# A column mean whose last row groups are added by another split of the engines: group 61 by GpSimd and TensorE, and VectorE held behind a store

## The chip, the cores, the metric

One core of one Trainium2 chip. The metric is the device time of one execution in microseconds; every kernel here computes the mean of each column of an 8192 x 8192 fp32 array.

## The reference

```python
def setup_inputs():
    return {"x": np.random.randn(8192, 8192).astype(np.float32)}

def reference(x):
    return np.mean(x, axis=0)
```

## The kernel before

The rows form 64 groups of 128; a group is a tile of 128 partitions and 8192 columns. Five engines work side by side: SyncE issues the loads into four row buffers, VectorE adds groups into `acc`, at the end TensorE sums over the partitions by multiplying with a tile of 1/8192, GpSimd takes over some late additions, and ScalarE copies sums out. The columns are 16 blocks of 512 (`F`); TensorE's sums of blocks 0 to 14 go to four banks of PSUM (the memory into which it adds), the last, the "edge", to a tile of its own. "Landed" means that all semaphore signals of a transfer have come; a "record" is one instruction's entry in the trace. For the last three groups the work is shared out, so that little is left to do when the last bytes land:

```python
    add(acc[:, 6 * F:], acc[:, 6 * F:], r61[:, 6 * F:], [load(r61[:, 4 * F:], rows(g)[:, 4 * F:])])  # VectorE
    g += 1
    load(r62, rows(g))
    tc.keep_in_program_order(nc.gpsimd.tensor_add(                                                  # GpSimd
        out=acc[:, 13 * F:], in0=acc[:, 13 * F:], in1=r62[:, 13 * F:]))
    g += 1
    for lo, hi in [(0, 9), (9, 12), (15, 16)]:
        load(r63[:, lo * F:hi * F], rows(g)[:, lo * F:hi * F])

    plan = [                      # TensorE, in this order: source, from block, to block
        (ahead, 12, 15),          # group 63, loaded early
        (acc, 0, 6),
        (head, 0, 4),             # group 61, loaded early
        (r61, 4, 6),
        (acc, 6, 13),             # waits for VectorE's part of 61
        (r62, 0, 13),
        (acc, 13, 16),            # waits for GpSimd's part of 62
        (r63, 0, 9),
        (r63, 9, 12),
        (r63, 15, 16),
    ]
    # ... one matmul per block; block i goes to column group i % 4 of the array and to bank i // 4

    copy(res[:96, 3, :], banks[3][:96, :])                       # ScalarE
    s3 = store(nc.scalar, out[12 * F:15 * F]..., res[0:96:32, 3, :], loads[-3])
    for b in range(3):
        copy(res[:, b, :], banks[b][:])                          # ScalarE
    nc.vector.tensor_copy(out=resedge[:], in_=edge[:])           # VectorE
    # ... SyncE waits for the loads
    store(nc.sync, out[:8 * F]..., res[0:P:32, 0:2, :])          # SyncE's first store: banks 0 and 1
    # ... SyncE waits for s3 and the last loads
    store(nc.sync, out[8 * F:12 * F]..., res[0:P:32, 2, :])      # SyncE's last store: bank 2
    store(nc.scalar, out[15 * F:]..., resedge[0:P:32, :])        # the edge store
```

Of the kernel before, what the change touches and what calls it, by code (L numbers as in the profile page):

```python
# [9 lines left out]
def kernel(  # L10
# [2 lines left out]
    x: bass.AP,  # L13
    out: bass.AP,
):




# [17 lines left out]
    nc = tc.nc  # L37
    f32 = mybir.dt.float32
    M, N = x.shape
    P = nc.NUM_PARTITIONS  # L40
    F = 512
# [4 lines left out]
    sync = mybir.DependencyInfo(mybir.DependencyClass.Sync, mybir.DependencyReason.DATA)  # L46
# [6 lines left out]
    acc = bufs[:, U - 1, :]  # L53
# [18 lines left out]
    def load(dst, src):  # L72
        ins = tc.keep_in_program_order(nc.sync.dma_start(out=dst, in_=src)).ins
        k = len(loads)
        over = loads[k - 8:k - 6] if k >= 8 and k % 2 == 0 else []
        tc.declare_no_dep(ins, group="loads", keep=over, reason="the reader of the buffer waited")
        for o in over:
            tc.add_manual_dep(ins, o.name, sync, reason="covers the next load too")
        tc.add_to_no_dep_group("loads", ins)
        loads.append(ins)  # L80
        return ins

    def rows(g, n=1):
        return x[g * P:(g + n) * P, :]

    def load_rows(g, u, n):
        return load(bufs[:, u:u + n, :], rows(g, n).rearrange("(p j) c -> p j c", j=n))
# [3 lines left out]
    def add(dst, a, b, dmas):  # L91

        ins = nc.vector.tensor_add(out=dst, in0=a, in1=b).ins  # L93
        if dmas and adds:
            waiter = nc.scalar if len(adds) % 8 > 1 else nc.gpsimd
            nop = joins[waiter] = tc.keep_in_program_order(waiter.nop()).ins  # L96
            for o in dmas + adds[-1:]:
                tc.add_manual_dep(nop, o.name, sync, reason="the no-op waits")
            for group in ("loads", "adds"):
                tc.declare_no_dep(ins, group=group, reason="the no-op waited")  # L100
            tc.add_manual_dep(ins, nop.name, sync, reason="waits for both at once")
        elif adds:
            tc.declare_no_dep(ins, group="loads", reason="the add ahead waited")
        tc.add_to_no_dep_group("adds", ins)
        adds.append(ins)
# [9 lines left out]
    g = 6  # L115
    while g < G - 10:
        u = (g + 2) % 4
        dma = load_rows(g, u, 2)
        add(both, bufs[:, u, :], bufs[:, u + 1, :], [dma])
        add(acc, acc, both, [])  # L120
        g += 2
    while g < G - 3:
        row = bufs[:, (g + 2) % 4, :]
        add(acc, acc, row, [load(row, rows(g))])
        g += 1
    r61, r62, r63 = [bufs[:, (g + 2 + j) % 4, :] for j in range(3)]
    add(acc[:, 6 * F:], acc[:, 6 * F:], r61[:, 6 * F:], [load(r61[:, 4 * F:], rows(g)[:, 4 * F:])])
    g += 1
    load(r62, rows(g))
    tc.keep_in_program_order(nc.gpsimd.tensor_add(  # L130
        out=acc[:, 13 * F:], in0=acc[:, 13 * F:], in1=r62[:, 13 * F:]))
    g += 1
    for lo, hi in [(0, 9), (9, 12), (15, 16)]:
        load(r63[:, lo * F:hi * F], rows(g)[:, lo * F:hi * F])

    plan = [
        (ahead, 12, 15),
        (acc, 0, 6),
        (head, 0, 4),
        (r61, 4, 6),  # L140
        (acc, 6, 13),
        (r62, 0, 13),
        (acc, 13, 16),
        (r63, 0, 9),
# [5 lines left out]
    for row, lo, hi in plan:  # L150
        base = 12 * F if row is ahead else 0
        for i in range(lo, hi):
            for q in range(4) if i == NBLK else [i % 4]:
                c = i * F + (q * W if i == NBLK else 0)
                dst = edge if i == NBLK else banks[i // 4]
                tc.keep_in_program_order(nc.tensor.matmul(  # L156
                    out=dst[32 * q:32 * q + 32, :],
# [10 lines left out]
    resedge = sb.tile([P, W], f32, name="resedge")  # L168
# [4 lines left out]
    def store(engine, dst, src, *then):  # L173
        ins = tc.keep_in_program_order(engine.dma_start(out=dst, in_=src)).ins
        for o in then:
            tc.add_manual_dep(ins, o.name, sync, reason="follows that load")
        return ins
# [12 lines left out]
    landed(loads[-2], s3)  # L190
    landed(loads[-1], adds[-1])
    store(nc.sync, out[8 * F:12 * F].rearrange("(q c) -> q c", q=4), res[0:P:32, 2, :])
    store(nc.scalar, out[15 * F:].rearrange("(q c) -> q c", q=4), resedge[0:P:32, :])


# [28 lines left out]
```

## Time and profile before

| | before |
|---|---|
| time | 630.02 us (median of 6 runs, 629.82 to 630.25) |
| span of the profile | 628.05 us |
| read from memory | 268.44 MB at 427 GB/s |
| VectorE's part of group 61 | 609.54 to 615.03 us |
| GpSimd's part of group 62 | 615.55 to 619.02 us |
| group 63, blocks 0 to 8, landed | 620.89 us |
| last store issued, landed | 624.57, 627.21 us |

All times inside an execution are us from the start of the span. The prediction below shows and reads the page, the chain and the timeline of this kernel. One part of the page it does not show, and that turned out to matter: the list of the DMA queues (packets, MB, share of the 16 engines' span).

### The profile page before, as it was taken

The numbers are of one execution on the slowest core, as the hardware profiler recorded it, in microseconds if no ns is written. First come the engines' busy times: TensorE is split into PE (matmuls) and PEld (weight loads), VectorE is DVE, ScalarE is ACT, GpSimd is POOL, SyncE is SP. The second block draws the span as 40 slices with busy tenths as digits, with TensorE's granted clock in tenths as the row PEclk, the third lists the DMA queues (packets, MB, share of the 16 engines' span).
The fourth block names the chain that finished last, engine by engine and source line by source line (L and its number), as shares of the span: only waits on it lengthen the run. The fifth ranks groups of instructions, "written<-read, shape, count | busy, mean of one in ns | idle before, by whom it ended". The sixth has DMA issues, their size and how long they took to land.

```text
span 628.1 us, 453 instructions
## 1 busy us (share of the span) xinstructions
PE 16.3 (3%) x114; PEld 5.7 (1%) x114; DVE 527.0 (84%) x60; ACT 3.7 (1%) x6; POOL 4.0 (1%) x7
## 2 busy tenths in 40 slices
PE   0000100000000000000000000000000000000017
PEld 0000000000000000000000000000000000000002
DVE  0019999999888998888988889888899888999991
ACT  0000000000000000000000000000000000000001
POOL 0000000000000000000000000000000000000002
PEclk9999999999999999999999999999999999999999
DMA  9999999999999999999999999999999999999996
GB/s 401 417 451 402 449 455 413 455 413 455 413 455 413 455 413 447 422 442 426 438 430 438 430 430 438 426 442 413 455 405 463 401 467 401 434 434 434 432 434 256
DMA packets 5924, 268.50 MB, mean 428 GB/s; under 512 B 655, under 2 KB 659, under 8 KB 1058
## 3 DMA queue, kind: packets, MB, share of 16 engines
q1 hardware_dynamic: 5908, 268.46, 99.0%
q8 instruction: 1, 0.02, 0.0%
q10 hardware_dynamic: 14, 0.01, 0.0%
q14 instruction: 1, 0.01, 0.0%
HBM read 268.44 MB, written 0.03 MB: 427 GB/s over the span
## 4 chain that ended last, share of the span: by engine, by line
DMA 55%; DVE 33%; another core or an unknown queue 10%; PE 0%; issue 0%; ACT 0%; ACTq 0%; POOLq 0%; POOL 0%
DMA bufs<-in_x_dram 55%; DVE bufs L93 33%; PE bank L156 0%; ACT bufs L171 0%; ACTq L96 0%; POOLq L96 0%; POOL ready L60 0%; POOL ones L57 0%; POOLq L208 0%
## 5 line engine op out<-in xcount | busy, mean ns | idle before, releaser
L93 DVE TENSOR_TENSOR bufs<-bufs 128x8192 f32<-128x8192 f32 (+2 forms) x59 | 526.7, 8927 | 88.3 <-DMA bufs<-in_x_dram 44.3
L156 PE MATMUL bank<-bufs,ones 128*32 128x512 f32 x84 | 12.7, 662 | 542.3 <-DVE bufs L93 542.0
L156 PEld LDWEIGHTS bank<-bufs,ones 128*32 128x32 f32 x84 | 4.2, 117 | 550.4 <-DVE bufs L93 544.4
L184 DVE COPY resedge<-edge 128x128 f32<-128x128 f32 x1 | 0.3, 291 | 9.1 <-PE edge L156 9.1
L130 POOL TENSOR_TENSOR bufs<-bufs 128x1536 f32<-128x1536 f32 x1 | 3.5, 3471 | 614.4 <-DMA bufs<-in_x_dram 614.4
L171 ACT COPY bufs<-bank 128x512 f32<-128x512 f32 (+1 forms) x4 | 2.2, 586 | 620.0 <-PE bank L156 620.0
L156 PE MATMUL bank<-ahead,ones 128*32 128x512 f32 x6 | 1.9, 1056 | 65.5 <-DMA ahead<-in_x_dram 65.5
L156 PE MATMUL bank<-head,ones 128*32 128x512 f32 x8 | 3.3, 990 | 0.0
L156 PE MATMUL edge<-bufs,ones 128*32 128x128 f32 x16 | 1.7, 274 | 0.0
L114 ACT ACT_TABLE_LOAD x1 | 1.3, 1283 | 0.7 <-PEq L208 0.7
L156 PEld LDWEIGHTS edge<-bufs,ones 128*32 128x32 f32 x16 | 1.0, 109 | 0.9 <-DMA bufs<-in_x_dram 0.5
L156 PEld LDWEIGHTS bank<-ahead,ones 128*32 128x32 f32 x6 | 0.2, 138 | 65.5 <-issue 65.5
L156 PEld LDWEIGHTS bank<-head,ones 128*32 128x32 f32 x8 | 0.6, 159 | 1.3 <-issue 1.3
L114 ACT COPY warm<-ones 128x32 f32<-128x32 f32 x1 | 0.2, 218 | 0.0
L60 POOL TENSOR_TENSOR ready<-ones 128x1 f32<-128x1 f32 x1 | 0.2, 193 | 0.1
L57 POOL MEMSET ones<- 128x32 f32 x1 | 0.1, 125 | 0.3 <-POOLq L208 0.3
L208 POOL MEMSET const-bfloat16-1.0<- 128x1 bf16 x1 | 0.1, 102 | 0.0
L208 POOL MEMSET const-uint8-127<- 128x1 uint8 x1 | 0.1, 102 | 0.0
L208 POOL MEMSET const-float32-0.0<- 128x1 f32 x1 | 0.1, 98 | 0.2 <-issue 0.2
L208 POOL MEMSET const-float32-1.0<- 128x1 f32 x1 | 0.1, 98 | 0.0
## 6 DMA issues: line engine op xcount, KB each, us to landing
bufs<-in_x_dram SPq DMA_DIRECT2D x8, 4096.0 KB, 22.3
bufs<-in_x_dram SPq DMA_DIRECT2D x1, 3072.0 KB
bufs<-in_x_dram SPq DMA_DIRECT2D x1, 2304.0 KB, 20.2
head<-in_x_dram SPq DMA_DIRECT2D x1, 1024.0 KB, 4.8
ahead<-in_x_dram SPq DMA_DIRECT2D x1, 768.0 KB
bufs<-in_x_dram SPq DMA_DIRECT2D x1, 768.0 KB, 21.7
bufs<-in_x_dram SPq DMA_DIRECT2D x26, 29.9
bufs<-in_x_dram SPq DMA_DIRECT2D x1, 256.0 KB, 21.9
```

Source lines behind the costliest of these rows:

```text
L57: nc.gpsimd.memset(ones[:], 1.0 / M)
L60: nc.gpsimd.tensor_add(out=ready[:], in0=ones[:, 0:1], in1=ones[:, 1:2]))
L93: ins = nc.vector.tensor_add(out=dst, in0=a, in1=b).ins
L114: tc.keep_in_program_order(nc.scalar.copy(out=warm[:], in_=ones[:]))
L130: tc.keep_in_program_order(nc.gpsimd.tensor_add(out=acc[:, 13 * F:], in0=acc[:, 13 * F:], in1=r62[:, 13 * F:]))
L156: tc.keep_in_program_order(nc.tensor.matmul(out=dst[32 * q:32 * q + 32, :], lhsT=ones[:], rhs=row[:, c - base:c - base + (W if i == NBLK e ...
L171: tc.keep_in_program_order(nc.scalar.copy(out=dst, in_=src))
L184: nc.vector.tensor_copy(out=resedge[:], in_=edge[:])
L208: nc = _bacc.Bacc("TRN2", target_bir_lowering=False, num_devices=1)
```

## The change

The intent: VectorE is free after group 60; GpSimd adds blocks 9 to 15 of group 61 and then, as before, its part of group 62; TensorE adds blocks 4 to 8 of group 61 directly. And VectorE's stream of instructions ends behind the store of the edge.

```diff
+    def late_add(row, lo):
+        tc.keep_in_program_order(nc.gpsimd.tensor_add(
+            out=acc[:, lo * F:], in0=acc[:, lo * F:], in1=row[:, lo * F:]))
...
-    add(acc[:, 6 * F:], acc[:, 6 * F:], r61[:, 6 * F:], [load(r61[:, 4 * F:], rows(g)[:, 4 * F:])])
+    load(r61[:, 4 * F:], rows(g)[:, 4 * F:])
+    late_add(r61, 9)
     g += 1
     load(r62, rows(g))
-    tc.keep_in_program_order(nc.gpsimd.tensor_add(
-        out=acc[:, 13 * F:], in0=acc[:, 13 * F:], in1=r62[:, 13 * F:]))
+    late_add(r62, 13)
...
-        (acc, 0, 6),
+        (acc, 0, 9),
         (head, 0, 4),
-        (r61, 4, 6),
-        (acc, 6, 13),
+        (r61, 4, 9),
+        (acc, 9, 13),
...
-    store(nc.scalar, out[15 * F:]..., resedge[0:P:32, :])
+    last = store(nc.scalar, out[15 * F:]..., resedge[0:P:32, :])
+    hold = tc.keep_in_program_order(nc.vector.nop()).ins
+    tc.add_manual_dep(hold, last.name, sync, reason="VectorE ends with the last store")
```

## The prediction

> **What bounds the kernel now.** I read the page first (busy table, slices, DMA queues), then the chain of waits, then the timeline of each engine in the last 30 us, since the change touches nothing earlier.
>
> ```profile
> span 628.1 us, 453 instructions
> PE 16.3 (3%) x114; PEld 5.7 (1%) x114; DVE 527.0 (84%) x60; ACT 3.7 (1%) x6; POOL 4.0 (1%) x7
> DMA  9999999999999999999999999999999999999996
> HBM read 268.44 MB, written 0.03 MB: 427 GB/s over the span
> ```
>
> The input is 8192 x 8192 x 4 bytes = 268.4 MB, read once. The DMA row is full until the last slice. VectorE is busy 84% and looks like the bound, but it is not: the chain of waits goes through transfers for 55% of the span and through VectorE for 33% only because a pair's two adds follow its landing. So only the tail can move: what lies between the last landings (620.9 to 623.4) and 628.1. The end of the chain:
>
> ```profile
> 600.66 20.22 DMA bufs<-in_x_dram
> 620.89 0.14 issue
> 621.02 2.90 PE bank L156 x24
> 623.92 0.02 issue
> 623.94 0.58 ACT bufs L171
> ```
>
> Columns are start, length, what. Blocks 0 to 8 of group 63 land at 620.89, TensorE adds them at once, ScalarE copies the last bank to 624.52; the two last stores, the ends and the final barrier make the other 3.5 us. This is the path that the change must shorten or may lengthen. Beside it, in the timeline:
>
> ```profile
> 591.94 23.09 DVE L93 TENSOR_TENSOR bufs<-bufs 128x8192 f32<-128x8192 f32 x3
> 615.55 3.47 POOL L130 TENSOR_TENSOR bufs<-bufs 128x1536 f32<-128x1536 f32 x1 [614.42 <-DMA bufs<-in_x_dram]
> 620.62 0.58 ACT L171 COPY bufs<-bank 96x512 f32<-96x512 f32 x1 [618.37 <-PE bank L156]
> 621.23 1.27 ACTq L174 DMA_DIRECT2D out_dram<-bufs  x1
> 622.54 1.07 ACT L171 COPY bufs<-bank 128x512 f32<-128x512 f32 x2 [1.34 <-PE bank L156]
> 623.94 0.58 ACT L171 COPY bufs<-bank 128x512 f32<-128x512 f32 x1 [0.32 <-PE bank L156]
> ```
>
> VectorE adds groups 59, 60 and then the part of 61, ending at 615.03. GpSimd adds three blocks and the edge of group 62 until 619.02; with it TensorE finishes bank 3, ScalarE copies that at 620.62, issues its store for 1.27 us, and reaches banks 0, 1 at 622.54, with no time in between. Before the last copy it has only 0.32 us of slack. So GpSimd's end stands some 0.4 us off the binding path, no more.
>
> [...] 3471/1536 = 2.26 ns a column against 5492/5120 = 1.07 (groups by form), a factor 2.1. [...] here the two never overlap, for VectorE's last add ends before GpSimd may start. [...] consecutive passes of one column group start 0.85 us apart at 609.5 to 613.8 and 0.43 us apart later, so the rate doubled some 4.5 us after the start. [...]
>
> **The change, part by part.**
>
> Removed: VectorE's one add of 5120 columns, 5.49 us (609.54 to 615.03). VectorE then ends with group 60 at 609.45. No load waits for the removed add (the last loads are issued at 601.5, and the built programs show the same waits on the queue), so no transfer starts earlier. Gain on the path: 0.
>
> Added on GpSimd: an add of 3584 columns (blocks 9 to 15) ahead of the old one. It may start when group 60 is added; group 61 landed at 605.7 (its semaphore). The old GpSimd add began 0.16 us after the last thing it waited for, so start 609.45 + 0.15 = 609.6. Duration: 3584 x 2.26 = 8.1 us with no fixed cost; less a fixed part, taken from the 193 ns of the one-column add, (3471 - 193) / 1535 = 2.14 ns a column and 0.2 + 7.65 = 7.85 us[...]. I take 7.85: end 617.45. The old add follows after a semaphore wait of about 0.1 us and takes 3.47 us: end **621.0 instead of 619.02**, 2.0 us later. VectorE did it in half the time; that is the heart of the matter.
>
> Added on TensorE: 3 blocks of acc and 3 of r61 more (18 instead of 12 before the long wait). Blocks go to four column groups that run side by side; the fullest has 6 blocks. Estimate: 2.65 blocks at 1.7 us until the rate doubles at 614, 3.35 at 0.86: idle by 616.9, before GpSimd's 617.5. Off the path. From 617.5 it must do acc 9 to 12 and the 13 blocks of r62: for the groups that hold blocks 13 and 14 that is 4 blocks, 3.45 us, ready at 620.95; so both arrive together with GpSimd at 621.07. In the kernel before these groups were free only at about 619.4 to 619.5, 0.4 us after GpSimd; that slack is used up. Two passes on, and 0.17 us of completion: bank 3 is done at 621.07 + 0.43 + 0.59 + 0.17, some 622.3. Column group 0 has five blocks, free at 621.8, edge to about 622.1: group 63, which had begun at 621.02, begins at 622.2. By the spacing of before (1.10, 1.96 and 2.8 us from that start to banks 0, 1, 2) the banks are done at 623.3, 624.2, 625.0; before, 622.1, 623.0, 623.9. TensorE alone makes +1.1 us.
>
> ScalarE: copy of bank 3 at 622.3 instead of 620.62 (+1.7), store issued at 622.9. If the issue again takes 1.27 us, the copies of banks 0 and 1 start at 624.2 and 624.7, end at 625.3, and SyncE's first store follows at 625.3 instead of 623.64; it takes 0.70, the waits behind it 0.22, and the last store starts at 626.2 instead of 624.57: **+1.66 us**. If the issue takes only 0.6 us, as the same queue's second store did, TensorE sets the pace: copies end at 624.8, the last store starts at 625.7: +1.15 us. Behind it landing (2.64 us from issue) and barrier stay as they are.
>
> The hold on VectorE: no instruction of its own; the built program puts the wait on VectorE's last branch. The edge store landed at 627.03, SyncE's last at 627.21, and SyncE goes on to 627.34 before the barrier fires. VectorE must be released and drained by then; it has 0.3 us and drains took 0.01 to 0.03 us. After the change the edge store goes out earlier still against the last one. Worth 0, give or take 0.2.
>
> Sum: 0 + (1.15 to 1.66) + 0 us, I take **+1.5 us: 630.2 + 1.5 = 631.7 us**, slower by a quarter of a per cent.
>
> **The rivals.** First, GpSimd stays hidden: the tail is set by the landing of group 63 alone, and the time is 630.2. For it speaks that the chain names only the transfer ahead of TensorE; against it that the slack is 0.4 us and the shift 2.0. Second, TensorE falls back to half rate in its idle stretch from 616.9 to 617.5 (for some column groups from 616). Then the work from 617.5 doubles: the groups reach block 13 at 624.4 rather than 620.95, and the time is near 635. [...] Third, the hold costs or gives something behind the barrier, where the profile shows nothing: the measured 630.2 is 2.1 us over the span. I see no mechanism for more than some tenths.
>
> **Range and chances.** The low end is the hidden case plus a little, 630.6; the high end +1.66 with GpSimd 0.3 us slower, a late doubling and the difference between chips, 633.0. Two per cent are 12.6 us, and the whole tail behind the last landing is under 5: faster 0.01, slower 0.01, within 2% 0.98.
>
> **What would show it.** GpSimd's wide add at 609.6 for about 7.85 us, its narrow one ending near 621.0; the bank 3 copy at 622.3 with GpSimd, not TensorE's backlog, as the last wait; the ACT store's issue length; group 63's matmuls starting at 622.2 although it still lands at 620.9; the last store at 625.7 to 626.2; a span of 629.2 to 629.7. Wrong if that last store starts within 0.3 us of 624.57, if the passes behind 617.5 are 0.85 us apart, or if the span and the time move by different amounts.

The sum came to 0 + (1.15 to 1.66) + 0 us, taken as +1.5, and the 7.85 us of the wide add rest on the trace's 2.14 ns a column. One term of the range is 0.3 us for a late doubling, an estimate from no run, which the high end of 633.0 counts in. In the paragraph that begins with 3471/1536, the 2.26 ns a column are GpSimd's and the 1.07 VectorE's. Of the second rival's premise, that TensorE's rate can fall to half again, the trace of before shows one case: its clock record stands at 1.00 from 614.12 to 627.77 and at 0.50 behind, 3.7 us after TensorE's last pass ended (624.10). Whether an idle stretch of 0.6 us, as forecast here, is enough it does not show.

## More of the kernel before

```profile
q1 hardware_dynamic: 5908, 268.46, 99.0%
q8 instruction: 1, 0.02, 0.0%
q10 hardware_dynamic: 14, 0.01, 0.0%
q14 instruction: 1, 0.01, 0.0%
```

Two packets are of the kind that the page names `instruction`, no data; they are read here as an engine's fetches of its instructions. They count for nothing in the shares. When they run is not on the page. By the trace's packet records q8's runs from 622.18 to 623.28, before the last two stores move; q14's is the one that matters below.

## The result, and the profile after

The changed kernel takes **630.41 us** (median of 6 runs, 630.21 to 630.79), the kernel before 630.02 in the same rounds: 0.39 us more, where 1.5 were predicted; the predicted range began at 630.6. Ratios in this document are the mean time of one kernel's fast runs over that of the other's in the same rounds, so not quite the ratio of the medians; here it is 1.0007, 95% interval 0.9994 to 1.0020. By the time alone the two kernels are not told apart. Their traces, however, differ in two large steps of opposite sign.

The first step is the predicted one. Groups by form of the kernel after (columns: line, engine, operation, tiles, form, count, then busy us and mean ns, then idle us before it):

```profile
L123 POOL TENSOR_TENSOR bufs<-bufs 128x3584 f32<-128x3584 f32 x1 | 7.8, 7770 | 608.5 <-DVE bufs L92 608.5
L123 POOL TENSOR_TENSOR bufs<-bufs 128x1536 f32<-128x1536 f32 x1 | 3.5, 3471 | 0.1
```

They run from 609.60 to 620.91, as predicted to a tenth. ScalarE's part of the timeline of the kernel after (start, length):

```profile
622.07 0.58 ACT L175 COPY bufs<-bank 96x512 f32<-96x512 f32 x1 [619.82 <-PE bank L160]
622.68 1.27 ACTq L178 DMA_DIRECT2D out_dram<-bufs  x1
624.00 1.56 ACT L175 COPY bufs<-bank 128x512 f32<-128x512 f32 x3 [1.34 <-PE bank L160]
```

Bank 3 is copied at 622.07 instead of 620.62, the store behind it is issued for the same 1.27 us, and the three other copies now follow each other without a gap. The chain of the kernel after names TensorE, where the chain before named the transfer:

```profile
600.83 8.70 DVE bufs L92
609.53 0.04 issue
609.57 11.73 PE bank L160 x69
...
622.24 1.76 PE bank L160 x12
624.00 0.91 ACT bufs L175 x2
624.90 0.05 issue
624.96 0.60 ACT bufs L175
```

It does so because TensorE is hardly idle from 609.57 on; which of its waits matters the chain doesn't say (pool_late and pe_part bear on it). SyncE's last store, in the timelines of before and of after:

```profile
624.57 0.56 SPq L174 DMA_DIRECT2D out_dram<-bufs  x1
```

```profile
626.01 0.56 SPq L178 DMA_DIRECT2D out_dram<-bufs  x1
```

It is issued 1.45 us later. So far the prediction holds (1.15 to 1.66). But the span grew by 0.53 us only (628.05 to 628.59), and the barrier behind the store costs the same. The second step is the landing, counted from a store's issue to its last semaphore signal: the store issued at 624.57 landed at 627.21, that at 626.01 landed at 627.74, 2.64 against 1.72 us (from unrounded times, as in the table below). The edge store before took 2.55 us to land, after 1.82. The DMA queues in the 0.8 us in which the parts of these last two stores move, before (625.6 to 626.4) and after (626.7 to 627.5), show what shares the engines with them:

```profile
q14 instruction: 1, 0.01, 3.9%
q1 hardware_dynamic: 8, 0.01, 3.5%
q10 hardware_dynamic: 8, 0.00, 1.2%
```

```profile
q1 hardware_dynamic: 10, 0.01, 3.6%
q10 hardware_dynamic: 8, 0.00, 1.3%
```

q1 carries SyncE's store, q10 the edge store, q14 an instruction fetch of 8192 bytes. Before, it runs from 625.68 to 626.18, in the midst of the stores: by the packet records three of the edge store's four parts start at 625.71 to 625.73, the fourth at 626.18, when the fetch is done. Its semaphore arrives 0.82 us after its last packet, the last store's 0.91 us; after the change these are 0.38 and 0.33. So where the fetch runs, one part of the edge store starts late and both semaphores come late. What delays the semaphores is not shown; which of the 16 engines carried which packet the packed trace does not tell. After the change, the fetch starts at 628.63, when the stores have landed and the span (628.59) has just ended.

### The profile page after: what moved, and what is told of

It reads as the page before. It is cut to its first block, busy times and chain, and to the rows that moved or that the text cites. A ratio compares the mean times of both kernels' runs of the same rounds, so it can differ in the third digit from the quotient of the medians.

```text
span 628.6 us, 466 instructions
## 1 busy us (share of the span) xinstructions
PE 17.4 (3%) x120; PEld 5.7 (1%) x120; DVE 521.5 (83%) x59; ACT 3.6 (1%) x6; POOL 11.8 (2%) x8
## 4 chain that ended last, share of the span: by engine, by line
DMA 52%; DVE 35%; another core or an unknown queue 10%; PE 2%; ACT 0%; issue 0%; ACTq 0%; POOLq 0%; POOL 0%
DMA bufs<-in_x_dram 52%; DVE bufs L92 35%; PE bank L160 2%; ACT bufs L175 0%; ACTq L95 0%; POOLq L95 0%; PE edge L160 0%; POOL ready L59 0%; POOL ones L56 0%; POOLq L214 0%
## 5 line engine op out<-in xcount | busy, mean ns | idle before, releaser
L92 DVE TENSOR_TENSOR bufs<-bufs 128x8192 f32<-128x8192 f32 (+1 forms) x58 | 521.2, 8986 | 88.3 <-DMA bufs<-in_x_dram 44.3
L160 PE MATMUL bank<-bufs,ones 128*32 128x512 f32 x90 | 15.2, 694 | 542.0 <-DVE bufs L92 542.0
L123 POOL TENSOR_TENSOR bufs<-bufs 128x3584 f32<-128x3584 f32 (+1 forms) x2 | 11.2, 5620 | 608.5 <-DVE bufs L92 608.5
```

Source lines behind the costliest of these rows:

```text
L92: ins = nc.vector.tensor_add(out=dst, in0=a, in1=b).ins
L123: tc.keep_in_program_order(nc.gpsimd.tensor_add(out=acc[:, lo * F:], in0=acc[:, lo * F:], in1=row[:, lo * F:]))
L160: tc.keep_in_program_order(nc.tensor.matmul(out=dst[32 * q:32 * q + 32, :], lhsT=ones[:], rhs=row[:, c - base:c - base + (W if i == NBLK e ...
```

## The experiments

Theory A, formed from the two traces: VectorE's end triggers the fetch some 1.4 us later (by the records, 1.2 us behind the edge copy before and 1.3 us behind the waiting branch after), and the hold moves it behind the stores. The rivals were B, that the stores landed late before only because they were issued 0.09 us apart (after: 0.60); C, that the hold does nothing; D, that any held engine shortens the final barrier. Each run is compared with runs of the kernel before on the same chip. The landings, from the semaphore records of the one profiled execution of each kernel, in us:

| kernel | last store issued | landed after | edge store landed after | fetch begins | span |
|---|---|---|---|---|---|
| before | 624.57 | 2.64 | 2.55 | 625.68 | 628.05 |
| after | 626.01 | 1.72 | 1.82 | 628.63 | 628.59 |
| hold_only | 624.43 | 1.95 | 1.65 | 627.16 | 627.34 |
| split_only | 625.89 | 1.71 | 1.83 | 629.07 | 628.77 |
| early_end | 624.63 | 1.70 | 1.81 | 628.14 | 627.83 |
| hold_gpsimd | 625.26 | 2.62 | 3.04 | 626.36 | 628.73 |
| pad2 | 624.76 | 2.03 | 1.66 | 466.22 | 627.64 |
| pad1 | 625.18 | 2.02 | 1.65 | 476.34 | 628.04 |
| hold_mid | 624.30 | 2.03 | 1.65 | 626.50 | 627.18 |
| pool_late | 626.03 | 1.72 | 1.84 | 628.44 | 628.60 |
| pe_part | 625.08 | 1.94 | 1.65 | 627.71 | 627.88 |

### hold_only: the hold alone on the kernel before

```diff
-    store(nc.scalar, out[15 * F:]..., resedge[0:P:32, :])
+    last = store(nc.scalar, out[15 * F:]..., resedge[0:P:32, :])
+    hold = tc.keep_in_program_order(nc.vector.nop()).ins
+    tc.add_manual_dep(hold, last.name, sync, reason="VectorE ends with the last store")
```

> The kernel before with the hold alone. Theory A (VectorE's end starts an 8192-byte instruction fetch some 1.4 us later; in the kernel before it runs at 625.68 to 626.18[...]): the fetch moves behind the last store, the edge store lands about 1.8 us and SyncE's last store about 1.75 us after its issue (at 626.3 both), the span is 0.8 us shorter, the time about 629.2. Rival B (the short landings in the changed kernel come from the two stores being issued 0.6 us apart there and only 0.09 us apart before): issues stay 0.09 us apart, landings stay at 2.55 and 2.64 us, the time stays at 630.0. Rival C (the hold does nothing): 630.0.

Measured: 629.26 us (5 runs, 629.21 to 629.71) against 630.09 (9 runs, 629.75 to 630.42); ratio 0.9989, interval 0.9977 to 1.0002, which just takes in 1; but no run of the one is as long as any of the other. Of the 0.71 us by which the span is shorter, the earlier issue of the last store in this execution makes 0.14, the landing 0.69, and 0.11 is lost again behind it, at the barrier, where VectorE now comes later than SyncE. The queues between 625.5 and 626.2, where the parts of the last two stores move:

```profile
q1 hardware_dynamic: 8, 0.01, 3.9%
q10 hardware_dynamic: 8, 0.00, 1.4%
```

No fetch is there, and the stores land in 1.65 and 1.95 us though they are still issued 0.07 us apart. C has fallen. B has fallen as the main cause but keeps a remnant: with stores this close together the last one takes 1.94 to 2.03 us in every kernel of the table that has no fetch there; where it follows some 0.6 us behind the edge store, or precedes it, it takes 1.70 to 1.72. So of the 0.92 us that the changed kernel's last store won, 0.6 to 0.7 go to the fetch (2.64 less 1.94 to 2.03) and the rest, 0.2 to 0.3, to the spacing. The spacing was compared between kernels, not varied alone.

### split_only: the change without the hold

```diff
-    last = store(nc.scalar, out[15 * F:]..., resedge[0:P:32, :])
-    hold = tc.keep_in_program_order(nc.vector.nop()).ins
-    tc.add_manual_dep(hold, last.name, sync, reason="VectorE ends with the last store")
+    store(nc.scalar, out[15 * F:]..., resedge[0:P:32, :])
```

> The change without the hold. Theory A: last store issued near 626.0 as with the hold, but the fetch comes some 1.4 us after VectorE's end at 625.4, at 626.8 to 627.3, among the parts of the last stores: landing 2.4 to 2.7 us, span 629.2 to 629.6, time 631.0 to 631.5, slower than before by 1.0 to 1.5 us. Rival B (spacing of the stores): landing 1.75 us, span 628.6, time 630.4, the same as with the hold.

Measured: 630.77 us (5 runs, 630.49 to 630.82) against 630.09; ratio 1.0010, interval 0.9997 to 1.0023. A miss for theory A as it stood. VectorE ended at 625.3 without a hold, but the fetch did not come at 626.8, nor did it meet a store: it came at 629.07, when the span (628.77) was over. In its place something else was lost. At the final barrier all engines drain, wait, and drain again; the records of SyncE's and VectorE's drains (count, ns min/median/max, first and last start) are, without and with the hold:

```profile
L223 SPq DRAIN  x3: 7/7/7, 627.7 to 628.0; - x3
L223 DVEq DRAIN  x2: 144/234/325, 625.0 to 628.4; - x2
```

```profile
L225 SPq DRAIN  x3: 7/7/7, 627.8 to 628.1; - x3
L225 DVEq DRAIN  x2: 10/14/17, 627.5 to 628.1; - x2
```

Without the hold VectorE's second drain comes 0.4 us behind SyncE's (628.41 and 627.98) and takes 144 ns; with it they come together. From SyncE's arrival at the barrier to the end of the span pass 1.03 us here, against 0.71 in the kernel before and in the changed one. The fetch's packet cannot be what holds the drain up, for it starts 0.66 us behind it.

### early_end: VectorE ends early, without a hold

```diff
-    nc.vector.tensor_copy(out=resedge[:], in_=edge[:])
+    copy(resedge[:], edge[:])        # ScalarE
```

> The kernel before with the edge copied by ScalarE, so that VectorE ends at 615.0 and needs no hold. Theory A: the fetch comes near 616.5, long before the stores; it may hold one load up by a few tenths. The edge is copied behind bank 2, 0.3 us later, its store is issued near 624.85 and lands at 626.7 (1.8 us), SyncE's last store lands at 626.3: span 627.5 to 627.7, time 629.4 to 629.7 in spite of the later edge. Rival C: nothing gained and the edge store 0.35 us later: 630.0 to 630.4.

Measured: 629.96 us (629.80 to 630.27) against 630.09; ratio 0.9999, interval 0.9987 to 1.0012. Theory A missed again: the fetch came at 628.14, behind the span's end (627.83), though VectorE had nothing to do from 615.1 on. The stores landed early, and VectorE's second drain again came 0.43 us behind SyncE's; from SyncE's arrival to the end pass 1.04 us, so that a third of a microsecond of the gain is lost there. VectorE's *end* is not the trigger.

### hold_gpsimd: another engine held

```diff
-    hold = tc.keep_in_program_order(nc.vector.nop()).ins
+    hold = tc.keep_in_program_order(nc.gpsimd.nop()).ins
```

(against hold_only)

> The kernel before with GpSimd held behind the last store in place of VectorE. Theory A: VectorE still ends at 624.5, the fetch still comes near 625.7, the last stores still land 2.5 to 2.7 us after their issue: 630.0, as before. Rival D (it is the barrier at the end that a held engine shortens, whichever it is): 629.2 or so here too.

Measured: 630.10 us (629.61 to 630.76) against 630.09; ratio 0.9998, interval 0.9984 to 1.0011. D has fallen. The queues between 625.9 and 626.9, among the last stores:

```profile
q1 hardware_dynamic: 11, 0.01, 3.6%
q14 instruction: 1, 0.01, 1.9%
q10 hardware_dynamic: 8, 0.00, 1.2%
```

The fetch stays, and the stores take 2.62 and 3.04 us (the profile is of the slowest of the five runs, its last store issued 0.7 us later than in before). The packets repeat the pattern of before: three parts of the edge store start by 626.05, the fourth at 626.66, as the fetch ends at 626.67, and both semaphores come 1.01 us after the last packet.

**Theory A2.** In these six traces the fetch is tied to a place in VectorE's stream. It starts 1.1 to 1.7 us after the end of VectorE's 63rd record, whatever that record is: in before and hold_gpsimd (66 records) the first drain at the end, in hold_only (67) the branch that waits, in after (66; one add less, one waiting branch more) the first drain, which is behind the hold, and in split_only and early_end (65) the wait inside the barrier. And where no wait hides it, the record that follows comes some 0.5 us later instead of 0.1, which costs time where the barrier is just then waiting for VectorE: that is the late second drain. The packet starts 0.6 to 0.7 us behind this late record, so it is a mark of the place and not what delays the record; what does stays open. That the fetch is VectorE's own is inferred from this tie. By the theory, dropping or adding one instruction anywhere ahead moves the place by one. It was made from the traces that it explains; the next two runs test it, and the four later runs with a hold keep to it (67 records, the branch, a fetch 1.1 us after its end).

### pad2 and pad1: one or two more instructions, no hold

```diff
+    pad = sb.tile([P, 1], f32, name="pad")      # placed ahead of VectorE's first add
+    for _ in range(2):                          # pad1: range(1)
+        tc.keep_in_program_order(nc.vector.memset(pad[:], 0.0))
     loads = []
```

(against before)

> The kernel before, no hold, with two memsets of one column ahead of VectorE's first add, where it is idle. Theory A2 (from the first four runs: the fetch is bound to a place in VectorE's instruction stream, behind its 63rd record, and starts about 1.15 us after VectorE gets there): the 63rd record becomes the add of group 61, the fetch comes between 610.7 and 616.2, far from the stores, the edge store and the last store land 1.65 to 1.95 us after their issue, VectorE's steps at the barrier follow each other within 0.15 us, span 627.2 to 627.6, time 629.1 to 629.5, faster than before by 0.6 to 0.9 us without any hold. [...] Rival E (the hold itself, or the order of arrival at the barrier, is what shortens the landing): 630.0, landing 2.5 us and more.

Measured: 629.78 us (629.54 to 629.83) against 629.95 (9 runs, 629.64 to 630.05); ratio 0.9997, interval 0.9985 to 1.0010.

> The same with one memset. Theory A2: the 63rd record becomes the edge copy at 624.16, the fetch starts at 625.3 or so, still among the stores, 0.4 us earlier than before: the edge store is caught (landing over 2 us), the last store perhaps no longer; time between 629.3 and 630.1. If the two padded kernels do the same, the place in the stream is not the cause and A2 falls.

Measured: 629.80 us (629.47 to 629.96) against the same 629.95; ratio 0.9998, interval 0.9985 to 1.0010.

Both moved the fetch away from the stores, without any hold: rival E has fallen. But not to where it was expected. In pad2 it starts at 466.22, in the stretch from 465 to 468 beside a load:

```profile
q1 hardware_dynamic: 16, 1.05, 82.1%
q14 instruction: 1, 0.01, 0.7%
```

In pad1 it starts at 476.34. In both VectorE is then at its 47th record. So the fetch comes 16 records ahead of the 63rd (63 - 47) in both, and one add (10 us) apart. The 63rd record of before is a drain, which ended only when the work ahead had (at 624.50, the copy at 624.45; early_end's first drain lasts from 609.60 to 615.13, its last add to 615.08); with the pads it is an add or a copy. Whether that is why the fetch comes ahead of it, no run shows. A2 missed the place in both runs, and its own sign of being wrong, that the two padded kernels do the same, half came true (the same landings and times, the fetch one add apart). My expectation stood on VectorE getting to a place when it executes it.

The stores landed in 1.65 to 1.66 and 2.02 to 2.03 us, so the pads should have won 0.6 us; the time shows 0.15 to 0.17. The traces show where the rest went: just behind the fetch VectorE's adds, which wait for the loads, fall back by 0.35 us in pad2 (between the adds of 461.60 and 472.56) and by 0.98 in pad1 (480.75 and 492.35), and stay back to the end. In pad1 and in before, from 470 to 495:

```profile
492.35 8.69 DVE L97 TENSOR_TENSOR bufs<-bufs 128x8192 f32<-128x8192 f32 x1 [2.92 <-ACTq L100]
```

```profile
491.74 8.69 DVE L93 TENSOR_TENSOR bufs<-bufs 128x8192 f32<-128x8192 f32 x1 [1.94 <-ACTq L96]
```

The wait ahead of the add is 2.92 instead of 1.94 us. None of the other ten traces has such a step of over 0.1 us after 143 us. So a fetch among the loads is not free: in these two executions it cost more than half of what the landing won, or more than all of it.

### hold_mid: VectorE held behind SyncE's first store

```diff
-    store(nc.sync, out[:8 * F]..., res[0:P:32, 0:2, :])
+    mid = store(nc.sync, out[:8 * F]..., res[0:P:32, 0:2, :])
...
+    hold = tc.keep_in_program_order(nc.vector.nop()).ins
+    tc.add_manual_dep(hold, mid.name, sync, reason="VectorE ends with the first of SyncE")
```

(against before)

> The kernel before with VectorE held behind SyncE's first store, not the edge store. A2: the 63rd record is the branch, which comes at 625.5; the next drain follows 0.5 us later at 626.0, ahead of SyncE's at 626.5 and so off the path, and the fetch starts at 626.6, behind the last store's parts (626.05). Stores land in 1.65 to 1.95 us. Span 0.1 us shorter than with the hold behind the edge store (VectorE came 0.1 us behind SyncE there): 627.2, time 629.1 to 629.3. If the fetch still catches a store: 629.5 or more.

Measured: **628.99 us** (5 runs, 628.91 to 629.30) against 629.95; ratio 0.9987, interval 0.9975 to 1.0000. The slowest run is 0.34 us below the fastest of nine runs of before. In the trace VectorE passes the branch at 625.37, drains at 625.88, ahead of SyncE at 626.47, and the fetch begins at 626.50, behind the last store's packets. It has the lowest median of all versions and lies below both kernels. Against hold_only it was not run in the same rounds, and the ratios to before (0.9987 and 0.9989) do not part them; the traces have it 0.10 us shorter from SyncE's arrival at the barrier to the end (0.71 against 0.81).

### pool_part: GpSimd's part of the change with VectorE working beside it

```diff
-    add(acc[:, 6 * F:], acc[:, 6 * F:], r61[:, 6 * F:], [...])
+    add(acc[:, 6 * F:9 * F], acc[:, 6 * F:9 * F], r61[:, 6 * F:9 * F], [...])
+    tc.keep_in_program_order(nc.gpsimd.tensor_add(
+        out=acc[:, 9 * F:], in0=acc[:, 9 * F:], in1=r61[:, 9 * F:]))
...
-        (acc, 6, 13),
+        (acc, 6, 9),
+        (acc, 9, 13),
```

(against hold_only)

> The kernel before with the hold, and only GpSimd's part of the change: VectorE adds blocks 6 to 8 of group 61, GpSimd 9 to 15; TensorE adds what it added before. The prediction's step (GpSimd's end at 621.0 sets bank 3, and ScalarE behind it the last store): bank 3 copied at 622.1, last store issued near 626.0, 1.4 us later than with the hold alone, span 628.6, time 630.4 to 630.7. Rival (TensorE's six more blocks are what costs): bank 3 at 620.6 to 621.0, last store at 624.6 to 625.0, time 629.2 to 629.6. If VectorE's and GpSimd's adds overlap, GpSimd's wide add may show over 7.8 us.

Measured: 634.45 us (4 runs, 634.12 to 635.63) against 629.95; ratio 1.0078, interval 1.0063 to 1.0094. The run does not separate what it was made for, but shows something else. Groups by form:

```profile
L93 DVE TENSOR_TENSOR bufs<-bufs 128x1536 f32<-128x1536 f32 x1 | 9.4, 9354 | 0.1
L128 POOL TENSOR_TENSOR bufs<-bufs 128x3584 f32<-128x3584 f32 x1 | 7.8, 7762 | 608.2 <-DVE bufs L93 608.2
L132 POOL TENSOR_TENSOR bufs<-bufs 128x1536 f32<-128x1536 f32 x1 | 4.8, 4834 | 0.1
```

VectorE's add of 1536 columns, 1.6 us by its 1.07 ns a column, took 9.35 us: it started with GpSimd's wide add at 609.3 and ended at 618.66, 1.6 us after that ended at 617.05. GpSimd's next add took 1.36 us more than alone. GpSimd's wide add took 7.76 us, as without VectorE beside it (7.77 in the changed kernel). By these lengths the two did not advance together: VectorE's add ended as if it had begun when GpSimd's was done. What held it is not shown. So with adds of these sizes the change could not have given GpSimd its part while VectorE still added: blocks 6 to 8 had to go to TensorE.

### pool_late: GpSimd later, TensorE with less to do

```diff
-        out=acc[:, 13 * F:], in0=acc[:, 13 * F:], in1=r62[:, 13 * F:]))
+        out=acc[:, 11 * F:], in0=acc[:, 11 * F:], in1=r62[:, 11 * F:]))
...
-        (acc, 6, 13),  (r62, 0, 13),  (acc, 13, 16),
+        (acc, 6, 11),  (r62, 0, 11),  (acc, 11, 16),
```

(against hold_only)

> The kernel before with the hold; VectorE adds group 61 as before, GpSimd's add of group 62 takes 5 units (blocks 11 to 15) instead of 3, TensorE two blocks less. GpSimd starts at 615.5 with VectorE idle and takes 5.5 to 5.8 us (2560 columns), so it ends at 621.0 to 621.2 as in the changed kernel, while TensorE has less to do than in either. If GpSimd's end is what sets the path (the prediction's first step): bank 3 copied at 622.0 to 622.3, last store issued at 625.9 to 626.2, 1.5 us later than with the hold alone, span 628.6 to 628.9, time 630.5 to 630.8. If it is TensorE's number of blocks: 629.2, as with the hold alone.

Measured: 630.78 us (4 runs, 630.54 to 631.05) against 630.02 (7 runs, 629.79 to 630.35); ratio 1.0013, interval 0.9996 to 1.0030. Its timeline has the changed kernel's times:

```profile
615.29 5.60 POOL L130 TENSOR_TENSOR bufs<-bufs 128x2560 f32<-128x2560 f32 x1 [614.15 <-DMA bufs<-in_x_dram]
622.08 0.58 ACT L171 COPY bufs<-bank 96x512 f32<-96x512 f32 x1 [619.83 <-DMA bufs<-in_x_dram]
```

GpSimd ends at 620.89, bank 3 is copied at 622.08, the last store is issued at 626.03: within 0.02 us of the changed kernel (620.91, 622.07, 626.01), with five blocks fewer on TensorE than there (three of group 61, two of 62). GpSimd's end alone is enough for the whole delay.

### pe_part: TensorE's blocks alone

```diff
-    add(acc[:, 6 * F:], acc[:, 6 * F:], r61[:, 6 * F:], [...])
+    add(acc[:, 9 * F:], acc[:, 9 * F:], r61[:, 9 * F:], [...])
```

(against hold_only; with the changed kernel's plan)

> The kernel before with the hold; VectorE adds only blocks 9 to 15 of group 61 (3584 columns, 3.9 us, to 613.4), TensorE gets the six more blocks of the changed kernel, GpSimd is as before (615.5 to 619.0). If GpSimd's end sets the path, TensorE's blocks alone cost little: the fullest column group has 11 blocks from 609.5, which with the doubling at 614 to 614.9 end at 621.2 to 621.7 (estimate), group 63 starts by then instead of at 621.0, last store 0.2 to 0.7 us later than with the hold alone: time 629.4 to 629.9. If TensorE's blocks were the cause: 630.5 and more.

Measured: 629.79 us (629.43 to 629.89) against 630.02; ratio 0.9995, interval 0.9980 to 1.0010. In the profiled run blocks 0 to 8 landed at 621.33 and TensorE began with them at 621.46, 0.13 us later, as in the kernel before: its blocks delayed nothing there.

```profile
621.46 2.84 PE L156 MATMUL bank<-bufs,ones 128*32 128x512 f32 x24 [0.20 <-DMA bufs<-in_x_dram]
```

But TensorE had little to spare (its pass before that ended at 621.26), and by the trace's clock record its rate doubled at 612.98 here, at 615.07 in the changed kernel. Two more microseconds at half rate would have put it about 1.0 us back (an estimate from passes 0.85 and 0.43 us apart), past the landing. So the run does not show that the blocks cost nothing where the rate doubles late. (The record above speaks of six more blocks; three are more, of group 61, and three of `acc` are only taken earlier.) That landing is itself 0.4 us later than in before, and with it the last store; VectorE's adds run 0.4 us late from 143 us on, long before the change acts, so this is of the execution and not of the edit.

## Why the prediction was right and wrong

**The wide add on GpSimd: right.** 7.85 us predicted, 7.77 measured; GpSimd's end at 621.0 predicted, 620.91 measured.

**TensorE not at half rate again, and its backlog just hidden: right.** Its passes behind 617.4 are 0.43 us apart. The doubling came at 615.07, not 614; a late doubling was counted in at the high end of the range. It comes 3.07 us after TensorE's first pass of the tail in pe_part, 4.63 in before and 5.50 in the changed kernel, so the 4.5 us that the prediction read from one trace are one of a wide range. TensorE was ready for block 13 at 620.88 (passes at 620.45, the next 0.43 later), GpSimd's end was 620.91: they arrive together, as forecast. Group 63 began at 621.86 to 622.08, where 622.2 was forecast. "TensorE alone makes +1.1 us", the later end of bank 2 with GpSimd late, came out as 0.93 (624.81 against 623.88), less than ScalarE's 1.45 and so not the binding path.

**Bank 3, ScalarE and the last store: right.** 622.3 and +1.15 to +1.66 us predicted, 622.07 and +1.45 measured. The slack of some 0.4 us was right too: GpSimd ended 1.89 us later and the last store went out 1.45 later. pool_late shows that GpSimd's end alone is enough for this; that TensorE's backlog, which arrived with it, would not have done it alone is not shown.

**"Behind it landing (2.64 us from issue) and barrier stay as they are": wrong, and this is the failed step.** The landing is not a constant of a store. It fell to 1.72 us, while the barrier did stay (0.71 us in both). Of the 0.92 us, 0.6 to 0.7 are the fetch that no longer met the stores, 0.2 to 0.3 the wider spacing of the two last stores, which the delay itself brought. 1.45 - 0.92 = 0.53, the growth of the span, which ended at 628.59 and not at 629.2 to 629.7.

**"The hold on VectorE ... Worth 0, give or take 0.2 ... I see no mechanism for more than some tenths": wrong on the kernel before, and on other grounds in the changed one.** Alone it is worth 0.7 us by the ratio and 0.8 by the medians (hold_only). In the changed kernel it did not save the stores from the fetch: by split_only they were safe already, for VectorE's stream had become one add shorter and the fetch's place had moved behind them, to VectorE's wait inside the final barrier, where the late record cost 0.32 us (1.03 - 0.71). The hold added one record and so put the place back to VectorE's first drain, where nothing waits for the next record. That 0.32 comes from the traces; the times (630.41 with, 630.77 without, from different rounds) agree with it but their intervals overlap.

**The rivals.** The hidden case, 630.2, lies next to the measured time but was wrong in its mechanism: nothing was hidden, a loss and a gain met. That it came so near is luck. The third rival, the hold, named the right instruction and looked for its effect behind the barrier, where the profile shows nothing, and not in the DMA queues, where it does. Its "2.1 us over the span" sets the median of the time against the span of an execution that took 629.83; for that execution it is 1.8 us.

Open: why the fetch's place is this record and not another, and whether it is the same when the program is loaded otherwise; what delays VectorE's record there; whether fetch and store met on one DMA engine.

## What to carry to other kernels

When the tail of a kernel is a few microseconds, read the landing of each store, from its issue to its semaphore, and list what else is in the DMA queues then; one instruction fetch of 8 KB (0.50 us on the queues in before, 0.31 in hold_gpsimd) cost here 0.6 to 0.7 us, nearly half of what the moved additions cost, and adding or removing instructions on the engine to which it is tied moved it, not always to where it was wanted (among the loads it cost 0.35 and 0.98 us). In this kernel it paid to hold that engine behind a store that lands early enough to stay off the barrier (hold_mid: 628.99 against 629.95 us), rather than to move arithmetic: giving GpSimd seven tenths of VectorE's part cost 1.45 us on the path. And a difference near zero of a change with two parts calls for each part alone, before the sum is believed.
